# An encoder step on one core: the tiles whose v rows are gathered become 0 and 8, and the dense passes 1-3 and 4-7

## The chip, the cores and the metric

The kernel runs on one core of a Trainium2 chip. The metric is the device time of one execution in microseconds (us), the median of several runs. The profile is of one further execution of the same program.

## The reference, cut to what matters

One layer of a streaming encoder for 1024 prompt tokens and 64 sample tokens (the latter with 512 past ones), all in float32: a combined input projection, differential attention, multi-head latent attention (MLA), a gated merge, an output projection, and then a layer of single-neuron experts (PEER). The change concerns PEER. For each token it computes

```
s1, i1 = top_k(s[:, :, 0], 16); s2, i2 = top_k(s[:, :, 1], 16)
top, sel = top_k(s1[..., :, None] + s2[..., None, :], 16)
g = softmax(top)
act = gelu(einsum('td,thkd->thk', h, u[idx]))
out = einsum('thk,thkd->td', g * act, v[idx])
```

so that each token has 8 heads x 16 = 128 chosen experts out of 16384, a row of u (1024 numbers) for the dot product of each and a row of v for the weighted sum.

## The kernel before

Tokens are worked on in nine tiles: 0 to 7 are 128 prompt tokens each, tile 8 is the 64 sample tokens. Three groups (0 1 2, 3 4 5 and 6 7 8) run one after the other through projections, attention, MLA (48 units of a head and a tile in a group), the merge (w_b), w_out and PEER's scores (w_pq). Group 0 splits its matmul operands in two rounded halves; groups 1 and 2 run them in float32.

PEER's remaining work is cut into jobs, Python generators that give up control behind each step:

- route (28 steps): the top 16 of a tile's scores, on VectorE; writes the expert numbers and the gates to HBM.
- dots (128 steps, 64 for tile 8): per step one gather of 128 rows of u (`gather`, an indirect DMA that GpSimd issues, line 312) and one multiply-and-sum on VectorE (line 335). Ends with gelu and the weights (wgtd).
- build (33 steps): for a tile whose v is multiplied densely, one-hot products per eight tokens: two one-hot comparisons (375, 376) and two products on VectorE (384), eight scaled copies on ScalarE (381), 24 matmuls (391), two copies out of PSUM (395, 397). They make the tile's 128 x 16384 matrix of weights, in HBM (Ad), and for one tile (TR) 9 of 16 parts in SBUF (Ares). Each of its buffers has one copy.
- vg (128 or 64 steps): for a tile in VGATHER, per step one gather of 128 rows of v and one multiply-add on VectorE (line 426).

Jobs stand in two queues, r and d. `pump(us)` is called beside the matmuls (2.6 or 3.9 per projection piece; 1.1 to 1.16 times 1 + half the key blocks per attention or MLA unit; X) and gives each queue us x rate credits; a whole credit takes one step. So the rates set where in the program a step stands. Group 1 holds 577 us of pump (MLA 296 to 483, w_b to 515, w_out to 546, w_pq to 577), and group 2 holds 658 (q projection 140 to 172, attention to 292, MLA 323 to 564, then the same three); pass 0 holds 499. These positions are called credits below. The d queue starts in group 1 when tile 0 is routed, at 41.6. A group's routes come into the r queue at its end. The order in which each engine then runs its instructions is settled when the program is built, by `TileContext(nc, schedule_with_timeline_sim=True)`, in which the place in the program serves as priority, and an instruction that is ready can stand ahead of earlier ones that aren't. Gathers draw on four buffers of the pool gp and, while cur["more"] is set (from the end of group 0 to the end of group 2 in program order), on three more.

Behind the groups come two dense passes, over tiles 0 1 2 and 3 4 5 6. A pass reads all of v in 16 parts, splits each into two rounded halves (lines 1151, 1153), splits each tile's weights likewise (1165, 1166), and sums three products per tile in PSUM (line 1172). Pass 1 has four tiles, which fill all eight PSUM banks, so no build runs in it. `need` (line 1130) takes every step out of the queues up to the builds of the next pass. In program order the d queue runs: dots and build of tiles 0 to 6, dots of 8 and 7, v gathers of 8 and 7. The d rate is 0.42 in the groups and 1.0 in the passes. Each finished tile is normalised and stored by `finish`; the last v-gathered tile's finish stands at the very end (cur["late"]).

Of the kernel before, what the change touches and what calls it, by code (L numbers as in the profile page):

```python
# [20 lines left out]
D = 1024  # L21
# [11 lines left out]
MAGIC = float(0x5F3759DF)  # L33
MSC = 96.0 ** -0.5
GROUPS = ((0, 1, 2), (3, 4, 5), (6, 7, 8))
PASSES = ((0, 1, 2), (3, 4, 5, 6))
VGATHER = (8, 7)
GN = 384
SLOT = 3072
NW = 3  # L40
# [1 line left out]
PB = 5  # L42
NB = 8
RC = 9
TR = 6
RATE_D2, RATE_R2 = 1.0, 0.41
PUMP_G = (1.1, 1.113, 1.158)
RATE_D_G = (0.42, 0.42, 0.415)
RATE_R_G = (0.7, 0.7, 0.623)
DEPTH_DIFF = (3, 2, 2)  # L50
DEPTH_MLA = (2, 2, 2)
# [7 lines left out]
def hybrid_tile(ctx: ExitStack, tc: tile.TileContext, A):  # L59
# [3 lines left out]
    def ld(out, in_):  # L63
        if out.dtype == F32R:
            out = out.bitcast(F32)
        if in_.dtype == F32R:
            in_ = in_.bitcast(F32)
        return SP.dma_start(out, in_)
# [68 lines left out]
    def tr(t):  # L137
        return 128 if t < 8 else 64
# [166 lines left out]

    def gather(src, idx):
        gturn[0] += 1
        if cur["more"] and gturn[0] % 7 % 2:
            gb = cur["more"].tile([128, D], F32, name="gm", tag="gm")
        else:  # L310
            gb = cur["gp"].tile([128, D], F32, name="gb", tag="gb")
        G.indirect_dma_start(out=gb, out_offset=None, in_=src, in_offset=bass.IndirectOffsetOnAxis(ap=idx, axis=0))  # L312
        return gb
# [4 lines left out]
    def dots_job(t):  # L318
        ns = 128 if t < 8 else 64
        eidx = bp.tile([128, 128], I32, name="beidx")  # L320
        gk = bp.tile([128, 128], F32, name="bgk", tag="bgk")
        h2 = bp.tile([128, D], F32, name="h2r")
        if t < 8:
            ld(eidx, eidxd[t])
            ld(gk, gkd[t])
            ld(h2, h2d[t * 128:t * 128 + 128])
        else:
            ld(eidx[:, :64], packed(eidxd[8]))
            ld(gk[:, :64], packed(gkd[8]))
            src = h2d[NP:]  # L330
            ld(h2, bass.AP(tensor=src.tensor, offset=src.offset, ap=[[0, 2], [D, 64], [1, D]]))
        act = bp.tile([128, 128], F32, name="act")
        for k in range(ns):
            gb = gather(A["peer_u"], eidx[:, k:k + 1])
            V.scalar_tensor_tensor(gb, gb, 1.0, h2, op0=ALU.mult, op1=ALU.mult, accum_out=act[:, k:k + 1])  # L335
            yield
        wgt = act
        S.activation(wgt[:, :ns], act[:, :ns], AF.Gelu)
        V.tensor_tensor(wgt[:, :ns], wgt[:, :ns], gk[:, :ns], op=ALU.mult)
        ld(wgtd[t, :, :ns], wgt[:, :ns])  # L340

    def build_job(t):
        src = bp.tile([128, 3, 128], F32, name="bsrc", tag="oh1")
        ld(src[:, 0, :], wgtd[t])
        ld(src[:, 1:3, :], efd[t])
        p = cur["ps"].tile([128, 512], F32, name="mm")
        pv = p.rearrange("p (a n) -> p a n", n=128)
        for i in range(3):
            PE.transpose(pv[:, i, :], src[:, i, :], ident)
        ixT = bp.tile([128, 2, 128], BF16, name="ixT")  # L350
        S.copy(ixT, pv[:, 1:3, :])
        aT = bp.tile([128, 128], F32, name="aT")
        S.copy(aT, pv[:, 0, :])
        a3 = bp.tile([128, 3, 128], BF16, name="a3")
        a3f = bp.tile([128, 128], F32, name="a3f")
        for i in range(3):
            V.tensor_copy(a3[:, i], aT)
            if i == 0:
                V.tensor_copy(a3f, a3[:, 0])
            if i < 2:  # L360
                V.tensor_tensor(aT, aT, a3[:, i], op=ALU.subtract)
        yield
        shp = [128, 4, 128, 2]
        iv = iota2[:, None, :, :].to_broadcast(shp)

        def over(row, tt):
            return row[:, tt:tt + 8].rearrange("p (g x) -> p g x", x=2)[:, :, None, :].to_broadcast(shp)

        n = RC if t == TR else 0
        for t0 in range(0, 128, 16):  # L370
            stage = bp.tile([128, 16, 4, 8, 4], F32, name="stage", tag="stage")
            for tt in range(t0, t0 + 16, 8):
                oh1 = bp.tile(shp, BF16, name="oh1", tag="oh1")
                oh2 = bp.tile(shp, BF16, name="oh2")
                V.tensor_tensor(oh1, iv, over(ixT[:, 1], tt), op=ALU.is_equal)  # L375
                V.tensor_tensor(oh2, iv, over(ixT[:, 0], tt), op=ALU.is_equal)  # L376
                w3 = bp.tile([128, 3] + shp[1:], BF16, name="w3")
                for i in range(3):
                    if i == 0:
                        for x in range(8):  # L380
                            S.activation(w3[:, 0, x // 2, :, x % 2], oh2[:, x // 2, :, x % 2], AF.Copy,  # L381
                                         scale=a3f[:, tt + x:tt + x + 1])
                    else:
                        V.tensor_tensor(w3[:, i], oh2, over(a3[:, i], tt), op=ALU.mult)  # L384
                for q in range(2):
                    p = cur["ps"].tile([128, 512], F32, name="mm")
                    pv = p.rearrange("p (a n) -> p a n", n=128)
                    for j in range(4):
                        x = 4 * q + j
                        for i in range(3):  # L390
                            PE.matmul(pv[:, j, :], lhsT=oh1[:, x // 2, :, x % 2], rhs=w3[:, i, x // 2, :, x % 2],  # L391
                                      start=i == 0, stop=i == 2)
                    pc = p.rearrange("p (t c i) -> p c i t", t=4, i=8)
                    if n:
                        S.copy(cur["Ares"][:, :, (tt + 4 * q) // 4], pc[:, :n])
                    if n < 16:
                        S.copy(stage[:, n:, (tt - t0) // 4 + q], pc[:, n:])
                    yield
            ld(Ad[t, :, n:, t0 // 4:t0 // 4 + 4], stage[:, n:])

    def finish(acc, nr, t):
        if t in VGATHER:
            y = gp.tile([128, D], F32, name="y", tag="gb")
        else:
            y = cur["p2"].tile([128, D], F32, name="y", bufs=1)
        row_norm(y[:nr], acc[:nr], cur["gfin"], D, y[:nr])
        ld(out_rows("y", t), y[:nr])

    def vgather_job(t):
        while "p2" not in cur:  # L410
            yield
        ns = 128 if t < 8 else 64
        eidx = bp.tile([128, 128], I32, name="beidx")
        wgt = bp.tile([128, 128], F32, name="vwgt", tag="bgk")
        acc = cur["p2"].tile([128, D], F32, name="gacc", bufs=1)
        if t < 8:
            ld(eidx, eidxd[t])
            ld(acc, x1d[t * 128:t * 128 + 128])
        else:
            ld(eidx[:, :64], packed(eidxd[8]))  # L420
            V.memset(acc[64:128], 0.0)
            ld(acc[0:64], x1d[NP:])
        ld(wgt[:, :ns], wgtd[t, :, :ns])
        for k in range(ns):
            gb = gather(A["peer_v"], eidx[:, k:k + 1])
            V.scalar_tensor_tensor(acc, gb, wgt[:, k:k + 1], acc, op0=ALU.mult, op1=ALU.add)  # L426
            yield
        if t == 8:
            oth = cur["gp"].tile([128, D], F32, name="gb", tag="gb")
            ld(oth[0:64], acc[64:128])  # L430
            V.tensor_tensor(acc[0:64], acc[0:64], oth[0:64], op=ALU.add)
        if t == VGATHER[-1]:
            cur["late"] = lambda: finish(acc, tr(t), t)
        else:
            finish(acc, tr(t), t)

    def route_job(t, s_of):
        nr = tr(t)
# [97 lines left out]
        V.reciprocal(gs[:nr], gs[:nr])  # L536
        V.tensor_tensor(gk[:nr], gk[:nr], gs[:nr, :, None].to_broadcast([nr, H, 16]), op=ALU.mult)
        ld(gkd[t, :nr], gk[:nr].rearrange("p h k -> p (h k)"))
        if t not in VGATHER:
            queues["d"] += [(("dots", t), dots_job(t)), (("build", t), build_job(t))]  # L540
        elif t not in GROUPS[-1]:
            queues["d"].append((("dots", t), dots_job(t)))
        if t == max(x for x in GROUPS[-1] if x < 8):
            for v in [x for x in VGATHER if x in GROUPS[-1]]:
                queues["d"].append((("dots", v), dots_job(v)))
            for v in VGATHER:
                queues["d"].append((("vg", v), vgather_job(v)))

    for g, tiles in enumerate(GROUPS):
        cur["g"] = g  # L550
# [550 lines left out]
        gctx.close()  # L1101
        if g == 0:
            wctx.close()
            cur["more"] = ph1.enter_context(tc.tile_pool(name="gm", bufs=3))
    cur["more"] = None
    ph1.close()
    p2 = ctx.enter_context(tc.tile_pool(name="p2", bufs=2, reuse_waits="tile"))
# [16 lines left out]
    gfin = p2.tile([128, D], F32, name="gfin", bufs=1)  # L1124
    ld(gfin, bcast_rows(A["norm_final"], D))
    cur["gfin"] = gfin

    def need(tiles):
        for t in tiles:
# [158 lines left out]
```

## Time and profile before

| | |
|---|---|
| median of 3 runs | 4605.68 us (4603.78 to 4608.89) |
| the profiled execution | 4599.36 us, of which the span is 4597.6 us |
| mean granted TensorE clock | 0.873 |
| busy: TensorE, VectorE, ScalarE, GpSimd | 3811.5, 3301.5, 1680.1, 1993.2 us |
| gathers | 1280, of which 192 of v |

PE is TensorE (PEld its weight loads), DVE VectorE, ACT ScalarE, POOL GpSimd. A busy time is that of at least one instruction running. PEclk is the granted TensorE clock as a share of 2.4 GHz. Lines are those of the kernel; times in a stretch count from the start of the span.

### The profile page before, as it was taken

The page shows a single profiled execution, that of the slowest core. Times are in us where ns is not written, and L with a number is a line of the kernel's source. Part 1 is how long each engine was busy: PE and PEld are TensorE (multiplying, and loading weights), DVE is VectorE, ACT ScalarE, POOL GpSimd, SP SyncE. Part 2 cuts the span into 40 slices and gives each one's busy share as a digit, 9 for nine tenths or more (in the row PEclk, how much of TensorE's full clock was granted, in tenths as well). Part 3 has the DMA queues.
Part 4 walks back from the last instruction along what each step waited for, and adds up shares of the span by engine and source line. Part 5 has one row for each costly group of instructions (what it writes and reads, how often), then busy time and mean ns, then how long its engine had stood idle before and what let it go on. Part 6 is the DMA issues. An engine that isn't in the chain of part 4 may idle for free. (4 is left out here: it accounts for less than half of the span.)

```text
span 4597.6 us, 56297 instructions
## 1 busy us (share of the span) xinstructions
PE 3811.5 (83%) x19017; PEld 2989.6 (65%) x19017; DVE 3301.5 (72%) x7224; ACT 1680.1 (37%) x3720; POOL 1993.2 (43%) x1353
## 2 busy tenths in 40 slices
PE   6998988986776798887759977799999546999996
PEld 6977886645555575655536755577777435888885
DVE  4043457977889624797867886399997887777886
ACT  3344631124244522125613442335545453223231
POOL 3412331555777200233455554014465446555553
PEclk9967999977787898988759988899999757999998
DMA  5421245997989533788888789669988988998996
GB/s 174 172 84 57 75 164 191 354 346 263 357 302 336 183 118 121 245 299 290 270 276 277 263 276 311 207 226 324 339 288 298 314 286 287 351 336 308 354 345 227
DMA packets 467592, 1183.16 MB, mean 257 GB/s; under 512 B 45352, under 2 KB 218888, under 8 KB 452584
## 3 DMA queue, kind: packets, MB, share of 16 engines
q0 software_dynamic: 184320, 671.17, 41.4%
q1 hardware_dynamic: 282984, 508.41, 32.0%
q8 instruction: 150, 2.46, 0.2%
q14 instruction: 138, 1.13, 0.1%
HBM read 1074.60 MB, written 104.56 MB: 256 GB/s over the span
## 5 line engine op out<-in xcount | busy, mean ns | idle before, releaser
L312 POOL DMA_INDIRECT gb<-in_peer_u,beidx x917 | 1267.9, 1383 | 1632.0 <-DVE gb L335 708.1
L335 DVE SCALAR_TENSOR_TENSOR gb<-gb,h2r 128x1024 f32<-128x1024 f32 x917 | 1109.2, 1219 | 251.6 <-DMA gb<-in_peer_u,beidx 231.3
L1172 PE MATMUL acc_ps<-vlo,ahi 128*128 128x512 f32 x1792 | 562.8, 397 | 17.2 <-DVE vlo L1153 17.1
L1172 PE MATMUL acc_ps<-vhi,alo 128*128 128x512 f32 x1792 | 563.3, 396 | 14.9 <-DVE alo L1166 14.8
L1172 PE MATMUL acc_ps<-vhi,ahi 128*128 128x512 f32 x1792 | 559.8, 396 | 5.3 <-ACT ahi L1165 4.2
L391 PE MATMUL mm<-w,oh 128*128 128x128 bf16 x2688 | 255.7, 252 | 231.7 <-DVE oh L375 107.2
L1172 PEld LDWEIGHTS acc_ps<-vlo,ahi 128*128 128x128 f32 x1792 | 338.7, 191 | 93.2 <-DVE vlo L1153 24.2
L1172 PEld LDWEIGHTS acc_ps<-vhi,alo 128*128 128x128 f32 x1792 | 339.1, 190 | 88.7 <-DVE alo L1166 18.7
L1172 PEld LDWEIGHTS acc_ps<-vhi,ahi 128*128 128x128 f32 x1792 | 340.5, 191 | 78.3 <-ACT ahi L1165 6.0
L312 POOL DMA_INDIRECT gb<-in_peer_v,beidx x192 | 287.8, 1499 | 228.5 <-DVE gacc L426 159.0
L391 PEld LDWEIGHTS <-oh 128*128 128x128 bf16 x2688 | 209.6, 114 | 263.3 <-DVE oh L375 159.9
L1151 ACT CAST vhi<-vraw 128x1024 fp32r<-128x1024 f32 x256 | 265.6, 1053 | 192.4 <-DMA vraw<-in_peer_v 120.3
L312 POOL DMA_INDIRECT gm<-in_peer_u,beidx x171 | 220.8, 1291 | 256.0 <-DMA beidx<-eidxd 104.1
L166 PE MATMUL mm<-h,wraw 128*128 128x384 f32 (+1 forms) x1024 | 320.5, 474 | 13.5 <-ACT gt L696 11.2
L381 ACT ACTIVATE w<-oh,a3f 128x128 bf16<-128x128 bf16 x896 | 279.3, 428 | 102.4 <-DVE oh L376 62.5
L1153 DVE TENSOR_TENSOR vlo<-vraw,vhi 128x1024 fp32r<-128x1024 f32 x256 | 304.6, 1213 | 5.6 <-ACT vhi L1151 5.6
L426 DVE SCALAR_TENSOR_TENSOR gacc<-gb,vwgt,gacc 128x1024 f32<-128x1024 f32 x192 | 246.2, 1282 | 82.4 <-DMA gb<-in_peer_v,beidx 71.5
L178 POOL TENSOR_TENSOR wlo<-wraw,whi 128x2048 fp32r<-128x2048 f32 (+1 forms) x42 | 186.7, 4447 | 263.4 <-ACT whi L177 257.8
L166 PEld LDWEIGHTS mm<-h,wraw 128*128 128x128 f32 x1024 | 199.1, 196 | 130.1 <-issue 13.3
L1165 ACT CAST ahi<-araw 128x1024 fp32r<-128x1024 f32 x103 | 107.6, 1048 | 468.0 <-PE acc_ps L1172 402.8
L166 PE MATMUL mm<-wraw,h 128*128 128x256 f32 (+1 forms) x960 | 229.8, 395 | 33.3 <-ACT vt L689 33.1
L166 PEld LDWEIGHTS mm<-wraw,h 128*128 128x128 f32 (+1 forms) x960 | 176.5, 189 | 73.7 <-ACT vt L689 35.7
(381 smaller groups left out, 7199.3 us busy)
## 6 DMA issues: line engine op xcount, KB each, us to landing
vraw<-in_peer_v SPq DMA_DIRECT2D x256, 512.0 KB
wraw<-in_w_in SPq DMA_DIRECT2D x66, 1024.0 KB
araw<-Ad SPq DMA_DIRECT2D x103, 512.0 KB
Ad<-stage SPq DMA_DIRECT2D x48, 1024.0 KB
gb<-in_peer_u,beidx POOLq DMA_INDIRECT x917
wraw<-in_w_a SPq DMA_DIRECT2D x12, 1024.0 KB
wraw<-in_w_b SPq DMA_DIRECT2D x12, 1024.0 KB
wraw<-in_w_out SPq DMA_DIRECT2D x12, 1024.0 KB
```

The source lines that it names most:

```text
L166: PE.matmul(out, lhsT=L[0], rhs=R[0], start=start, stop=stop)
L178: G.tensor_tensor(lo[:, :n], raw[:, :n], hi[:, :n].bitcast(F32), op=ALU.subtract)
L312: G.indirect_dma_start(out=gb, out_offset=None, in_=src, in_offset=bass.IndirectOffsetOnAxis(ap=idx, axis=0))
L335: V.scalar_tensor_tensor(gb, gb, 1.0, h2, op0=ALU.mult, op1=ALU.mult, accum_out=act[:, k:k + 1])
L381: S.activation(w3[:, 0, x // 2, :, x % 2], oh2[:, x // 2, :, x % 2], AF.Copy, scale=a3f[:, tt + x:tt + x + 1])
L391: PE.matmul(pv[:, j, :], lhsT=oh1[:, x // 2, :, x % 2], rhs=w3[:, i, x // 2, :, x % 2], start=i == 0, stop=i == 2)
L426: V.scalar_tensor_tensor(acc, gb, wgt[:, k:k + 1], acc, op0=ALU.mult, op1=ALU.add)
L1151: S.copy(hi, raw)
L1153: V.tensor_tensor(lo, raw, hi.bitcast(F32), op=ALU.subtract)
L1165: S.copy(av, rv)
L1172: PE.matmul(pst[t][:, ds], lhsT=L[:, i, :], rhs=R[:, ds], start=c == 0 and i == 0 and L is ahi and R is vb[i][0], stop=c == 15 and i == 7 ...
```

## The change

Tile 0 is no longer built and multiplied densely; its v rows are gathered instead, and tile 7 changes places with it. Passes are over 1 2 3 and 4 5 6 7. Tile 0's v job is queued behind tile 3's build, with index and weight tiles of its own, and draws its sum from cur["more"]; all of it is taken out of the queue before the pools of the groups close. Its sum goes to x1d, and is read and finished at the head of the passes. Tile 8's dots and v gathers follow behind tile 7's build. The extra gather buffers are two instead of three, used by every third gather; the d rate is 0.56 in the groups and 1.3 in the passes. Before the build of TR (now 7) the r queue is emptied.

```
--- before.py
+++ after.py
@@ -33,8 +33,8 @@
 MAGIC = float(0x5F3759DF)
 MSC = 96.0 ** -0.5
 GROUPS = ((0, 1, 2), (3, 4, 5), (6, 7, 8))
-PASSES = ((0, 1, 2), (3, 4, 5, 6))
-VGATHER = (8, 7)
+PASSES = ((1, 2, 3), (4, 5, 6, 7))
+VGATHER = (0, 8)
 GN = 384
 SLOT = 3072
 NW = 3
@@ -42,10 +42,10 @@
 PB = 5
 NB = 8
 RC = 9
-TR = 6
-RATE_D2, RATE_R2 = 1.0, 0.41
+TR = 7
+RATE_D2, RATE_R2 = 1.3, 0.41
 PUMP_G = (1.1, 1.113, 1.158)
-RATE_D_G = (0.42, 0.42, 0.415)
+RATE_D_G = (0.56, 0.56, 0.56)
 RATE_R_G = (0.7, 0.7, 0.623)
 DEPTH_DIFF = (3, 2, 2)
 DEPTH_MLA = (2, 2, 2)
@@ -305,7 +305,7 @@
 
     def gather(src, idx):
         gturn[0] += 1
-        if cur["more"] and gturn[0] % 7 % 2:
+        if cur["more"] and gturn[0] % 3 == 1:
             gb = cur["more"].tile([128, D], F32, name="gm", tag="gm")
         else:
             gb = cur["gp"].tile([128, D], F32, name="gb", tag="gb")
@@ -340,6 +340,8 @@
         ld(wgtd[t, :, :ns], wgt[:, :ns])
 
     def build_job(t):
+        if t == TR:
+            drain("r")
         src = bp.tile([128, 3, 128], F32, name="bsrc", tag="oh1")
         ld(src[:, 0, :], wgtd[t])
         ld(src[:, 1:3, :], efd[t])
@@ -407,12 +409,10 @@
         ld(out_rows("y", t), y[:nr])
 
     def vgather_job(t):
-        while "p2" not in cur:
-            yield
         ns = 128 if t < 8 else 64
-        eidx = bp.tile([128, 128], I32, name="beidx")
-        wgt = bp.tile([128, 128], F32, name="vwgt", tag="bgk")
-        acc = cur["p2"].tile([128, D], F32, name="gacc", bufs=1)
+        eidx = bp.tile([128, 128], I32, name="veidx")
+        wgt = bp.tile([128, 128], F32, name="vwgt")
+        acc = (cur["more"] or cur["p2"]).tile([128, D], F32, name="gacc", tag="gacc", bufs=1)
         if t < 8:
             ld(eidx, eidxd[t])
             ld(acc, x1d[t * 128:t * 128 + 128])
@@ -429,10 +429,10 @@
             oth = cur["gp"].tile([128, D], F32, name="gb", tag="gb")
             ld(oth[0:64], acc[64:128])
             V.tensor_tensor(acc[0:64], acc[0:64], oth[0:64], op=ALU.add)
-        if t == VGATHER[-1]:
+        if t == 8:
             cur["late"] = lambda: finish(acc, tr(t), t)
         else:
-            finish(acc, tr(t), t)
+            ld(x1d[t * 128:t * 128 + 128], acc)
 
     def route_job(t, s_of):
         nr = tr(t)
@@ -536,15 +536,13 @@
         V.reciprocal(gs[:nr], gs[:nr])
         V.tensor_tensor(gk[:nr], gk[:nr], gs[:nr, :, None].to_broadcast([nr, H, 16]), op=ALU.mult)
         ld(gkd[t, :nr], gk[:nr].rearrange("p h k -> p (h k)"))
+        queues["d"].append((("dots", t), dots_job(t)))
         if t not in VGATHER:
-            queues["d"] += [(("dots", t), dots_job(t)), (("build", t), build_job(t))]
-        elif t not in GROUPS[-1]:
-            queues["d"].append((("dots", t), dots_job(t)))
-        if t == max(x for x in GROUPS[-1] if x < 8):
-            for v in [x for x in VGATHER if x in GROUPS[-1]]:
-                queues["d"].append((("dots", v), dots_job(v)))
-            for v in VGATHER:
-                queues["d"].append((("vg", v), vgather_job(v)))
+            queues["d"].append((("build", t), build_job(t)))
+        if t == PASSES[0][-1]:
+            queues["d"].append((("vg", 0), vgather_job(0)))
+        if t == 8:
+            queues["d"].append((("vg", 8), vgather_job(8)))
 
     for g, tiles in enumerate(GROUPS):
         cur["g"] = g
@@ -1101,7 +1099,9 @@
         gctx.close()
         if g == 0:
             wctx.close()
-            cur["more"] = ph1.enter_context(tc.tile_pool(name="gm", bufs=3))
+            cur["more"] = ph1.enter_context(tc.tile_pool(name="gm", bufs=2))
+    drain("r", ("route", PASSES[0][-1]))
+    drain("d", ("vg", 0))
     cur["more"] = None
     ph1.close()
     p2 = ctx.enter_context(tc.tile_pool(name="p2", bufs=2, reuse_waits="tile"))
@@ -1124,6 +1124,10 @@
     gfin = p2.tile([128, D], F32, name="gfin", bufs=1)
     ld(gfin, bcast_rows(A["norm_final"], D))
     cur["gfin"] = gfin
+
+    xr = p2.tile([128, D], F32, name="araw")
+    ld(xr, x1d[0:128])
+    finish(xr, 128, 0)
 
     def need(tiles):
         for t in tiles:
```

## Rows read from the trace of the kernel before

**Rows 1.** Head of the page.

```profile
span 4597.6 us, 56297 instructions
```

**Rows 2.** Stretch; busy (count) of PE, PEld, DVE, ACT, POOL; clock, DMA share, GB/s.

```profile
2970.00:3621.00 651.00, 601.94 (x3127) 482.58 (x3127) 586.03 (x1392) 310.47 (x542) 276.28 (x149) 0.96 0.86 297
3621.00:3846.00 225.00, 88.19 (x726) 72.25 (x725) 191.44 (x347) 111.83 (x333) 111.62 (x87) 0.56 0.89 294
3846.00:4562.00 716.00, 704.72 (x3074) 580.31 (x3072) 558.75 (x576) 193.53 (x189) 408.05 (x277) 0.99 0.91 329
```

**Rows 3.** The gathers (line 312) by stretch: GpSimd busy and count.

```profile
740.00:1561.00 821.00, 492.94 (x384) 0.80 0.87 316
1561.00:1886.00 325.00, 0.00 (x0) 0.95 0.34 117
1886.00:2884.00 998.00, 487.65 (x384) 0.84 0.83 284
2884.00:3052.00 168.00, 0.00 (x0) 0.88 0.58 189
3052.00:3532.00 480.00, 246.44 (x128) 0.97 0.90 315
3400.00:3500.00 100.00, 72.25 (x26) 0.97 0.89 310
3621.00:3846.00 225.00, 111.62 (x87) 0.56 0.89 294
3846.00:4050.00 204.00, 120.25 (x85) 0.98 0.93 338
4050.00:4562.00 512.00, 287.79 (x192) 0.99 0.90 325
```

**Rows 4.** First one-hots of the builds (line 375), 16 a build, by stretch.

```profile
1360.00:1570.00 210.00, 10.22 (x15) 0.76 0.84 297
...
3588.00:3731.00 143.00, 11.01 (x16) 0.70 0.92 315
3731.00:3846.00 115.00, 10.97 (x16) 0.51 0.85 277
```

**Rows 5.** The dots (line 335) from pass 0 to pass 1.

```profile
2970.00:3846.00 876.00, 282.21 (x467) 0.86 0.87 296
```

**Rows 6.** Ends of MLA units (line 926) by stretch, groups 1 and 2.

```profile
1290.00:1341.00 51.00, 3.21 (x12) 1.00 0.80 280
1341.00:1577.00 236.00, 5.06 (x19) 0.76 0.83 294
1577.00:1646.00 69.00, 4.49 (x17) 1.00 0.15 45
2448.00:2695.00 247.00, 10.30 (x42) 0.96 0.80 266
2695.00:2748.00 53.00, 1.44 (x6) 0.76 0.84 290
```

**Rows 7.** Busy time of all engines: three stretches of the groups' tails.

```profile
1561.00:1886.00 325.00, 300.18 (x1435) 218.32 (x1436) 120.32 (x527) 87.15 (x221) 0.00 (x0) 0.95 0.34 117
1646.00:1797.00 151.00, 142.09 (x570) 98.09 (x568) 37.76 (x164) 18.64 (x36) 0.00 (x0) 0.97 0.43 158
2768.00:2954.00 186.00, 145.15 (x732) 103.99 (x731) 96.32 (x198) 48.35 (x125) 54.40 (x40) 0.89 0.72 246
```

**Rows 8.** The q projection's copies (line 708), groups 1 and 2.

```profile
946.00:986.00 40.00, 3.79 (x8) 0.99 1.03 412
2014.00:2105.00 91.00, 3.48 (x8) 0.76 0.78 270
```

**Rows 9.** Ends of attention units (line 798) in group 2.

```profile
2105.00:2250.00 145.00, 4.04 (x12) 0.79 0.85 280
2250.00:2305.00 55.00, 2.12 (x6) 0.76 0.80 265
```

**Rows 10.** Section 5 of the page: the v gathers' accumulation.

```profile
L426 DVE SCALAR_TENSOR_TENSOR gacc<-gb,vwgt,gacc 128x1024 f32<-128x1024 f32 x192 | 246.2, 1282 | 82.4 <-DMA gb<-in_peer_v,beidx 71.5
```

More of the change, by code (lines that the diff above doesn't have):

```diff
@@ L35 @@
 GROUPS = ((0, 1, 2), (3, 4, 5), (6, 7, 8))
-PASSES = ((0, 1, 2), (3, 4, 5, 6))
-VGATHER = (8, 7)
+PASSES = ((1, 2, 3), (4, 5, 6, 7))
+VGATHER = (0, 8)
 GN = 384
@@ L44 @@
 RC = 9
-TR = 6
-RATE_D2, RATE_R2 = 1.0, 0.41
+TR = 7
+RATE_D2, RATE_R2 = 1.3, 0.41
 PUMP_G = (1.1, 1.113, 1.158)
-RATE_D_G = (0.42, 0.42, 0.415)
+RATE_D_G = (0.56, 0.56, 0.56)
 RATE_R_G = (0.7, 0.7, 0.623)
@@ L307, in gather @@
         gturn[0] += 1
-        if cur["more"] and gturn[0] % 7 % 2:
+        if cur["more"] and gturn[0] % 3 == 1:
             gb = cur["more"].tile([128, D], F32, name="gm", tag="gm")
@@ L342, in build_job @@
     def build_job(t):
+        if t == TR:
+            drain("r")
         src = bp.tile([128, 3, 128], F32, name="bsrc", tag="oh1")
@@ L409, in vgather_job @@
     def vgather_job(t):
-        while "p2" not in cur:
-            yield
         ns = 128 if t < 8 else 64
-        eidx = bp.tile([128, 128], I32, name="beidx")
-        wgt = bp.tile([128, 128], F32, name="vwgt", tag="bgk")
-        acc = cur["p2"].tile([128, D], F32, name="gacc", bufs=1)
+        eidx = bp.tile([128, 128], I32, name="veidx")
+        wgt = bp.tile([128, 128], F32, name="vwgt")
+        acc = (cur["more"] or cur["p2"]).tile([128, D], F32, name="gacc", tag="gacc", bufs=1)
         if t < 8:
@@ L431, in vgather_job @@
             V.tensor_tensor(acc[0:64], acc[0:64], oth[0:64], op=ALU.add)
-        if t == VGATHER[-1]:
+        if t == 8:
             cur["late"] = lambda: finish(acc, tr(t), t)
         else:
-            finish(acc, tr(t), t)
+            ld(x1d[t * 128:t * 128 + 128], acc)
     def route_job(t, s_of):
@@ L538, in route_job @@
         ld(gkd[t, :nr], gk[:nr].rearrange("p h k -> p (h k)"))
+        queues["d"].append((("dots", t), dots_job(t)))
         if t not in VGATHER:
[L540 to L547, printed above, removed]
+            queues["d"].append((("build", t), build_job(t)))
+        if t == PASSES[0][-1]:
+            queues["d"].append((("vg", 0), vgather_job(0)))
+        if t == 8:
+            queues["d"].append((("vg", 8), vgather_job(8)))
     for g, tiles in enumerate(GROUPS):
@@ L1103, in hybrid_tile @@
             wctx.close()
-            cur["more"] = ph1.enter_context(tc.tile_pool(name="gm", bufs=3))
+            cur["more"] = ph1.enter_context(tc.tile_pool(name="gm", bufs=2))
+    drain("r", ("route", PASSES[0][-1]))
+    drain("d", ("vg", 0))
     cur["more"] = None
@@ L1126, in hybrid_tile @@
     cur["gfin"] = gfin
+    xr = p2.tile([128, D], F32, name="araw")
+    ld(xr, x1d[0:128])
+    finish(xr, 128, 0)
     def need(tiles):
```

## The prediction, made before the changed kernel was run

> **What bounds the kernel now.** I read the span first [rows 1], then the engines' busy time by stretch for the part behind the three groups [rows 2], then where each kind of tail work (gathers, dots, builds) runs [rows 3 to 5], and last what a build costs the stage that it falls into [rows 6 to 9]. In rows 2 the reader is to see three stretches: the first dense pass (2970 to 3621 us), 225 us in which TensorE is busy for 88 us and no dense matmul can start, and the second pass (3846 to 4562), in which TensorE is busy for 704.7 of 716 us. The gap is made by order: the second pass takes all eight PSUM banks, so every build must be over, and the last two builds run from 3588 to 3846, a lone one in 115 us [rows 4]. Ahead of it VectorE is the fullest engine: 586.0 of 651 us and 191.4 of 225 us [rows 2]. Rows 3 show two stretches with no gather at all, 1561 to 1886 and 2884 to 3052: the dots of three tiles are done there and the next routing isn't. The 192 v gathers all lie in the second pass, beside TensorE's own work.
>
> **What the planner's order means.** Gathers run far ahead of their due place: by the credits, tile 2's dots are due in group 2 (its steps 322 to 449 of the d queue), and rows 3 have all 384 gathers of tiles 0 to 2 over by 1561. Builds stay at their due place: tile 0's is due at credits 346 to 425 of group 1's 577, and MLA holds credits 296 to 483; its one-hots run from 1360 to 1570 [rows 4], inside MLA's 1290 to 1646 [rows 6]. So I place moved builds by credits and moved gathers by the first idle stretch.
>
> **The change part by part.** The number of gathers, dots, builds and dense matmuls stays; seven tiles are built and passed densely before and after. What moves:
>
> (a) Tile 0's build leaves group 1's MLA. Rows 6: 12 units take 51 us with gathers and no build, 17 units take 69 us with neither, so about 4.1 us each; the 19 under the build take 236 us. 236 - 19 x 4.1 = 158, so -158 us. The granted clock tells the same: 1.00 before and behind, 0.76 under the build, between the two levels of 1.2 and 2.4 GHz, with TensorE waiting. The other bound is half of it, -80, if the saved time only lets other waits through.
>
> (b) Tile 1's build is now due at credits 499 to 558 of group 1 (rate 0.56: 128 dots to 270, 128 to 499, then 33 steps), which is w_b's second half, w_out and w_pq. The nearest rows are tile 2's build in the same place of group 2: the stretch from w_b to w_pq takes 186 us there and 151 us in group 1 without a build [rows 7], and the last six MLA units take 53 us for 6 x 5.9 [rows 6], 35 + 18 = 53. I take +55; bounds 0 (VectorE is busy 37.8 of 151 us there) and +115, a lone build.
>
> (c) In group 2, tile 1's build leaves the q projection and the first attention units: 91 us against 40 [rows 8], and 12 units in 145 us against 6 in 55 [rows 9], 12 x (12.1 - 9.2) = 35; together -86. Tile 2's build takes credits 209 to 268 there, some 11 of the 24 units: 11 x 2.9 = +32. Net -54.
>
> (d) Tile 2's build leaves group 2's tail, -53 as in (b); tile 3's comes, at credits 497 to 556, inside MLA (323 to 564), over 59 / 15.05 = 3.9 heads (15.05 credits each, of three units), 11.7 units. Priced as in (a), 236 / 19 - 4.1 = 8.3 us a unit: +97. Bounds +53 (as the old one) and +158. Net +44.
>
> (e) The 128 v gathers of tile 0 and their 128 accumulations, 1.282 us each [rows 10], 164 us of VectorE, move into the groups. Cover: 1561 to 1886 has no gather, and VectorE is busy 120.3 of 325 us [rows 7]. Their index and weight tiles have names of their own, so they wait for tile 0's dots alone and for gather buffers. They don't slow MLA (4.2 us with gathers, 4.1 without), but tile 1's build now stands there too. Bounds 0 and +164; I take +40, nearer the rows that show cover. One buffer fewer (six for seven) stretches 384 gathers from 821 us [rows 3] to at most 821 x 7 / 6 = 958, which still ends before tile 3's routing at 1886: nothing waits.
>
> (f) Before pass 1 may start, the dots of tiles 6 and 7 (256) and the builds of tiles 4 to 7 must now be over; before, it was tile 6 alone and builds 3 to 6, but 233 dots ran there in fact (467 records, two to a dot), 105 of them of tiles 8 and 7 as filler [rows 5]. So VectorE has at least 23 x 1.3 = 30 us more in a stretch where it is the fullest engine: +30. Bounds: 777 + 30 us at full use would fit in 807 of 876 us, -69; the other end is rival B, +132. With the rate at 1.3 all four builds are due inside pass 0 (credits 98 to 495 of 499), so part of the gap goes into a longer pass 0; that moves time and saves none by itself.
>
> (g) In pass 1, 277 gathers [rows 3] become 128 (tile 8's dots and v rows). TensorE is at 704.7 of 716 us, so -10, bounds 0 and -11. The tail behind the last matmul keeps five finishes; tile 0's finish moves to the head of pass 0, a load, some ten small operations and a store beside dense work: nothing, and about 5 us if pass 0 waits for its buffer.
>
> Sum: -158 + 55 - 54 + 44 + 40 + 30 - 10 = -53 us, on a span of 4597.6, a profiled execution of 4599.4 us (6.3 below the median of the runs): 4552.7 us on the median.
>
> **A rule weighed at (f).** Rows 3: in pass 0 the 128 gathers of tile 6 keep GpSimd busy 1.93 us each, and 2.78 us in the worst 100 us, against 1.28 in the groups and 1.50 in pass 1. The Trainium skill (SBUF — State Buffer, "Who interferes with whom") says that a VectorE instruction with two SBUF inputs contends with a GpSimd instruction that reads SBUF, which speaks against moving tile 7's gathers in among the splits of pass 0. By that rule at its worst row, 256 x 2.78 = 712 us from 3052, then a build of 115, pass 1 would start at 3879, +33 for (f). The pass-1 row, with the same splits beside it, speaks against its being the whole cause.
>
> **Rivals.**
> A, the forecast: builds leave MLA in group 1, the stretch before pass 1 grows little. 4553, its own range 4468 to 4595.
> B, slower: tile 7's dots gate pass 1. If tile 6's dots keep their 480 us from 3052 [rows 3] and tile 7's run at the gap's pace (225 / 87 = 2.59 us, 331 us), they end at 3863, the last build at 3978: +132 in place of +30, so -53 + 102 = +49, 4655 us. It decides once pass 1 starts over 83 us later against pass 0's start than now. For it: routing still holds VectorE early in pass 0. Against it: 105 of the dots there were filler, and the rate of 1.3 puts these ahead of dense work.
> C: the v gathers aren't pulled ahead of tile 3's dots, as both draw on the same buffers. The part is then not done in idle time: 128 x 998 / 384 = 333 us later in group 2, of which 2884 to 3052 hides 168; the other 165 us hold 63 dots of tile 5, 82 us of VectorE in pass 0, and the accumulations cost group 2 half of 164 for my 40: -53 + 82 + 42 = +71, 4677 us.
> D, no change: tile 3's build costs group 2's MLA what tile 0's cost group 1's (+158 for +97): -53 + 61 = +8, 4614 us.
>
> **How the numbers follow.** A has 0.55, B 0.22, D 0.15, C 0.08. The predicted time is A's. The range leaves about one in ten at each end: down to (e) at nothing and (f) at -15, 4468; up to C, 4675. A measurement of this kernel tells about 0.2%, 9 us, from no change: faster 0.55 is A, same 0.15 is D, slower 0.30 is B and C.
>
> **What would show each step.** (a): 48 MLA units of group 1 in some 200 us, at a granted clock near 1.0. (b), (d): one-hots of three builds in w_out and w_pq of group 1, in the attention and in the late MLA of group 2. (e): v gathers between about 1500 and 1900; after 2300 is C. (f): the time from pass 0's first dense matmul to pass 1's, 876 now: 906 by A, over 960 is B. (g): pass 1 near 706. I am wrong if group 1's MLA still takes 340 us, if the v gathers lie in group 2, or if VectorE in pass 0 waits for tile 7's gathers.

## The result and the profile after

The changed kernel takes 5026.0 us (median of 4 runs, 5012.3 to 5034.5) against 4607.1 for the kernel before: a ratio of 1.0907 [1.0879, 1.0936]. It is slower by 419 us, and the time lies far above the range that the prediction gave (4468 to 4675). The profiled execution has a span of 5032.7 us.

The busy time by stretch, cut at the first dense matmul, the end of pass 0, the start of pass 1 and the last matmul. The columns are those of [rows 2], to which these lines answer.

```profile
span 5032.7 us, 56375 instructions
...
2839.00:3430.00 591.00, 556.23 (x2523) 447.28 (x2523) 553.83 (x1352) 220.57 (x284) 300.88 (x174) 0.98 0.91 328
3430.00:4313.00 883.00, 164.60 (x1328) 138.23 (x1327) 632.55 (x1078) 205.55 (x590) 492.70 (x400) 0.51 0.83 276
4313.00:5020.00 707.00, 701.67 (x3077) 578.24 (x3076) 314.58 (x297) 193.54 (x192) 94.15 (x63) 1.00 0.50 176
```

The first dense matmul is at 2839 us, 138 earlier than before. Pass 1 came out at 707, as forecast. The loss is in the middle line: 883 us pass between the passes in place of 225, TensorE is busy for 165 of them, and its granted clock is 0.51 (0.56 before), close to the lower of its two levels.

Group 1's MLA units (the ends of units, line 924 here), the same before (line 926), and the first one-hots of builds (line 377 here) in the same stretch:

```profile
1288.00:1540.00 252.00, 12.49 (x47) 0.92 0.88 313
...
1291.00:1645.00 354.00, 12.49 (x47) 0.84 0.69 244
...
1288.00:1540.00 252.00, 0.00 (x0) 0.92 0.88 313
```

No build stands there any more, and the units take 252 us for 354.

The gathers (line 312) by stretch, beside [rows 3]:

```profile
740.00:1557.00 817.00, 492.26 (x384) 0.84 0.86 311
1557.00:1828.00 271.00, 0.07 (x1) 0.97 0.47 156
...
2155.00:2490.00 335.00, 173.32 (x132) 0.82 0.84 282
2490.00:2849.00 359.00, 1.25 (x1) 0.93 0.34 113
2849.00:3600.00 751.00, 396.98 (x249) 0.88 0.89 318
3600.00:4313.00 713.00, 396.60 (x325) 0.50 0.83 273
```

Two things stand here that the forecast didn't have. The v rows of tile 0 (128 of the 132) come at 2155 us, behind tile 3's dots; 1557 to 1828 stays without gathers. And there is a second stretch with none, 2490 to 2849, although tiles 4 and 5 have been routed by 2001 us. So 573 dots run between the first dense matmul and pass 1 (249 + 325 gathers), where before 233 did [rows 5].

What released GpSimd at 2849 is seen in the order of time (start, duration, engine and line, tiles, and in brackets the idle time before):

```profile
2836.84 1.06 ACT L202 ACTIVATE y<-araw 128x1024 f32<-128x1024 f32 x1 [1.47 <-DMA araw<-x1d]
...
2848.25 1.21 DVE L335 SCALAR_TENSOR_TENSOR gb<-gb,h2r 128x1024 f32<-128x1024 f32 x1
...
2849.73 0.94 POOL L312 DMA_INDIRECT gb<-in_peer_u,beidx  x1 [358.49 <-DVE Ares L445]
...
2859.91 0.34 SPq L68 DMA_DIRECT2D out_y_p<-y  x1
```

Only four gathers of tile 4 had been issued by 2490, and one of their dot products run. The next gather follows the second dot product, and that product follows the first write of y in tile 0's finish, at the head of the passes. In between VectorE is busy for 123 of 356 us (2492 to 2848) and runs none of these dots, so their place in the order that was settled at the build is behind the head of the passes. The page names a routing instruction as releaser; it shares nothing with the gather. What does share something is y: for a gathered tile it is taken from the gather buffers (tag "gb").

Last, what the engines waited for in the gap, 3430 to 4313 (total, times, longest):

```profile
PE mm L351 <- DMA bsrc<-wgtd: 447.2, 3, 153.6
```

Three builds wait for their dots' weights, 447 us in all. Before, over 3622 to 3846:

```profile
PE mm L349 <- DMA bsrc<-wgtd: 5.5, 1, 5.5
```

### The profile page after: what moved, and what is told of

It reads as the page before. It is cut to its first block, busy times and chain, and to the rows that moved or that the text cites. A ratio compares the mean times of both kernels' runs of the same rounds, so it can differ in the third digit from the quotient of the medians.

```text
span 5032.7 us, 56375 instructions
## 1 busy us (share of the span) xinstructions
PE 3786.3 (75%) x19017; PEld 2983.1 (59%) x19017; DVE 3326.4 (66%) x7224; ACT 1678.0 (33%) x3718; POOL 1928.6 (38%) x1353
## 4 chain that ended last, share of the span: by engine, by line
PE 24%; issue 11%; DVE 9%; DMA 8%; POOL 6%; ACT 2%; POOLq 0%; SPq 0%; ACTq 0%; DVEq 0%
PE acc_ps L1176 13%; POOL gb L312 6%; PE mm L166 4%; DMA gb<-in_peer_u,beidx 3%; DVE gb L335 3%; DMA Ad<-stage 2%; PE mm L919 1%; DVE vlo L1157 1%; DMA gb<-in_peer_v,veidx 1%; PE mm L393 1%; ACT w L383 1%; PE tp L725 1%; PE mm L794 1%; DVE alo L1170 1%; ACT stage L399 1%
## 5 line engine op out<-in xcount | busy, mean ns | idle before, releaser
L312 POOL DMA_INDIRECT gb<-in_peer_u,beidx x917 | 1232.4, 1344 | 1323.0 <-DVE gb L335 600.8
L393 PE MATMUL mm<-w,oh 128*128 128x128 bf16 x2688 | 275.7, 267 | 317.8 <-DVE oh L377 104.1
L393 PEld LDWEIGHTS <-oh 128*128 128x128 bf16 x2688 | 230.9, 121 | 361.6 <-DVE oh L377 183.0
L1155 ACT CAST vhi<-vraw 128x1024 fp32r<-128x1024 f32 x256 | 268.4, 1054 | 157.2 <-DMA vraw<-in_peer_v 78.3
L1170 DVE TENSOR_TENSOR alo<-araw,ahi 128x1024 fp32r<-128x1024 f32 x103 | 125.3, 1217 | 280.3 <-ACT ahi L1169 278.3
L312 POOL DMA_INDIRECT gb<-in_peer_v,veidx x149 | 208.1, 1397 | 164.4 <-DVE gacc L426 123.4
```

What stands on the lines that cost most here:

```text
L1155: S.copy(hi, raw)
L1170: V.tensor_tensor(alo.rearrange("p i (q t) -> p i q t", t=4), rv, av.bitcast(F32), op=ALU.subtract)
```

## The experiments

A time is set against the kernel before as run on the same chip; 1% is 46 us. Where two experiments are compared, their ratios to it are.

### The gather buffers and y

**e1**: y of tile 0 from a tag of its own in p2.

```
 def finish(acc, nr, t):
-    if t in VGATHER:
+    if t in VGATHER and t != 0:
```

> The changed kernel, but tile 0's finish takes its output tile y from the pass pool p2 (tag y, as the dense tiles do) and not from the gather ring gb. Theory 1 (ring order): the buffers of one tag are handed out in program order, y of tile 0 stands in the ring ahead of tile 4's gathers and can't be written before the groups' pools close, so the dots of tiles 4 and 5 wait for the passes; with y elsewhere they run in group 2 again, the stretch from the first dense matmul of pass 0 to that of pass 1 falls from about 1460 us to 850 to 950, and the time to 4560 to 4660. Theory 2 (VectorE load: the dots of tiles 6 and 7, at the rate of 1.3, gate pass 1 whatever the ring does): no gather moves, 4950 to 5030.

4785.8 us, 1.0413 [1.0377, 1.0448]: 4.9%, 227 us, are gone. Tile 4's 128 gathers now run in group 2, where the changed kernel had four:

```profile
2473.00:2777.00 304.00, 170.45 (x128) 0.83 0.82 268
```

It missed the expected time all the same, and the stretch from pass 0's first dense matmul to pass 1's is 1124 us, not 850 to 950: 187 us of loss stay, so y is about half of the answer.

**e2, e3**: the kernel before, with an extra finish of tile 0 at the head of the passes (its output is written once more at the end), with y from the gather buffers (e2) and from p2 (e3).

```
+    xr = p2.tile([128, D], F32, name="araw")
+    ld(xr, x1d[0:128])
+    y0 = gp.tile([128, D], F32, name="y", tag="gb")      (e2)
+    y0 = p2.tile([128, D], F32, name="y", bufs=1)        (e3)
+    row_norm(y0, xr, gfin, D, y0)
+    ld(out_rows("y", 0), y0)
```

> The kernel before, with one finish of tile 0 added at the head of the passes (load, norm, store; the rows are overwritten later by the real ones), whose y is taken from the gather ring gb. Nothing else moves. Theory 1: the gathers of tiles 4 and 5 (those that stand behind y) fall out of group 2, no gather from about 2300 to 2900, and the time goes up by 300 to 500 us, 4900 to 5100. Theory 2: within 15 us of the kernel before, 4595 to 4625.

> The same added finish of tile 0 in the kernel before, its y from the pass pool p2. It prices the added work alone. Theory 1 and theory 2 both: within 15 us of the kernel before; over 100 us slower would mean that the added load and norm at the head of the passes cost, not the ring.

e2 takes 5046.5 us (one run), 448 more than before; e3 takes 4597.1, 0.999 [0.9971, 1.001]. One tag in one line decides it. In e2 the gathers stop for 843 us and start again behind y:

```profile
2786.48 0.94 POOL L312 DMA_INDIRECT gb<-in_peer_u,beidx  x1 [843.10 <-DVE Ares L445]
```

Shown is that the shared tag holds back the dots behind it in the program until the head of the passes. That it does so because y can't be written before p2 opens is argued: how the build's scheduler ties the two is not read from the trace.

### The queue place of the v rows

**e4**: e1, with tile 0's v gathers alone on the two "gm" buffers and all u gathers on "gb".

```
...
+        if own:
+            gb = own.tile([128, D], F32, name="gv", tag="gm")
-        if cur["more"] and gturn[0] % 3 == 1:
+        elif not own_more and cur["more"] and gturn[0] % 3 == 1:
...
-            gb = gather(A["peer_v"], eidx[:, k:k + 1])
+            gb = gather(A["peer_v"], eidx[:, k:k + 1], cur["more"])
```

> As the run with y in p2, and tile 0's v gathers take the two extra buffers for themselves (u gathers keep the four of gb), so that they don't stand behind tile 3's gathers in a shared ring. Theory 1: the v gathers now run from about 1350 in group 1, where GpSimd idled from 1561 to 1886, and the time is 20 to 80 us below the run with y in p2, 4500 to 4620. Theory 2: 4950 to 5030, as the dots of tiles 6 and 7 are where they were.

4793.7 us, 1.0437 [1.0405, 1.0469], no better than e1. The v gathers spread over 764 to 1877 and the last gather of tile 2's dots is issued 315 us later than in e1: buffers taken from one are missing to the other. It tells nothing of the queue place.

**e8**: e1, with v queued ahead of tile 3's dots.

```
-        if t == PASSES[0][-1]:
+        if t == 2:
             queues["d"].append((("vg", 0), vgather_job(0)))
```

> e1 with one place changed: tile 0's v rows are queued ahead of tile 3's dots (behind tile 2's build) and not behind them, so that in the ring of gather buffers they come before tile 3's gathers. Theory (buffers are given out in the order of the program, and v behind tile 3's dots leaves GpSimd's queue idle from 1557 to 1828 us): the v gathers run in that stretch, each later tile's dots end 200 to 300 us earlier, tile 5's dots return to group 2, and the kernel takes 4620 to 4720 us. Rival (the v products only take VectorE's time from group 1 where it is needed, and the dots of tiles 6 and 7 gate pass 1 in any case): 4770 to 4800 us.

4724.0 us, 1.0262 [1.0225, 1.0298]: 1.5%, 69 us, better than e1, 4 us above the theory's range and well below the rival's. All 128 v gathers lie in the stretch that was empty, and tile 5's dots are back in group 2 (2587 to 2866):

```profile
1552.00:1850.00 298.00, 156.82 (x128) 0.83 0.92 331
```

The gain is small because the v rows cost the group something where they now stand (e13 to e15). The edit also moves something else: what is taken out of the queue before the passes ends with tile 0's v job, so tile 3's build is no longer among it. Its one-hots run from 2939 us, at the head of pass 0, and no longer from 2587, in group 2's MLA (e13 looks at its price).

### Tile 7's dots before pass 1

**e6** (on e1) and **e10** (on e8): tile 7's build takes weights of zero and its dots run behind it, so tile 7's routed part is missing from the output.

```
+    def blank_job(t):
+        act = bp.tile([128, 128], F32, name="act")
+        V.memset(act, 0.0)
+        ld(wgtd[t], act)
+        yield
-        queues["d"].append((("dots", t), dots_job(t)))
+        queues["d"].append((("dots", t), blank_job(t) if t == 7 else dots_job(t)))
+        if t == 7:
+            queues["d"].append((("late dots", t), dots_job(t)))
```

> The kernel after with tile 0's y in a buffer of its own (as in e1, 4786 us), and tile 7's expert dots taken out from in front of its build: the build uses weights of zero, and the same dots are worked out behind it, so tile 7's routed part is left out of the output while the gathers and VectorE's work stay the same. Theory (tile 7's dots, gathers first, gate its build and so pass 1): pass 1 starts 150 to 260 us earlier than e1's 4064 us, and the kernel takes 4540 to 4640 us. Rival (what is late is the sum of VectorE's and GpSimd's work, which is moved and not removed): pass 1 starts earlier and the end moves by under 50 us, 4740 to 4790 us.

> The two edits of e8 and e6 together, on top of e1's: y of tile 0 in its own buffer, tile 0's v rows ahead of tile 3's dots, and tile 7's dots behind its build, which uses weights of zero (tile 7's routed part is left out of the output, the work is the same). Theory (three separate costs make up the loss: the ring through y, 240 us; v behind tile 3's dots, 62 us; tile 7's dots before pass 1, 166 us): 4724 - 166 = 4558 us, so 4520 to 4600 us, and pass 1 starts near 3750 to 3860 us. Rival (with v early the dots of tile 7 no longer cost much, or the dots put behind delay the v rows of tile 8 to the same end): 4640 to 4720 us.

e6 takes 4619.7 us (one run), 166 less than e1, and pass 1 starts at 3885 for 4064. e10 takes 4597.2, 0.9991 [0.9965, 1.0016], 2.7% or 125 us less than e8, and pass 1 starts at 3851 for 4004. The wait of a build for its dots in the gap before pass 1, in e1, e8 and e10, in this order:

```profile
PE mm L351 <- DMA bsrc<-wgtd: 224.7, 2, 159.9
```

```profile
PE mm L351 <- DMA bsrc<-wgtd: 134.1, 1, 134.1
```

```profile
PE mm L357 <- DMA bsrc<-wgtd: 4.5, 1, 4.5
```

That tile 7's dots gate pass 1 is shown: 134 us of waiting taken away give 125. The edit also takes tile 7's 128 dot products out from before pass 1; that VectorE's time alone was short there is unlikely, since in e8's gap it is busy for 235 of 317 us, but no run separates the two:

```profile
3687.00:4004.00 317.00, 67.48 (x549) 55.42 (x547) 234.65 (x410) 88.32 (x264) 171.14 (x137) 0.52 0.83 276
```

Time before the passes and time at the gate add up only in part, though: e10 was to come near 4558 and is 39 above.

**e13**: e10 with group 2's pacing at 0.66, since e10's pass 0 begins with tile 3's build still running. Dense matmuls (tile acc_ps) in e10 at the head of pass 0, and the same in the kernel before:

```profile
2946.00:3062.00 116.00, 25.93 (x96) 18.94 (x95) 0.00 (x0) 0.63 0.56 183
3062.00:3160.00 98.00, 70.39 (x289) 55.21 (x290) 0.00 (x0) 0.84 0.89 318
```

```profile
2977.00:3095.00 118.00, 112.01 (x459) 89.51 (x460) 0.00 (x0) 0.93 0.70 235
```

> e10 (4597 us; y of tile 0 in its own buffer, its v rows early, tile 7's dots behind its build with weights of zero, so tile 7's routed part is left out of the output) with group 2's pacing at 0.66 for 0.56: tile 3's build stands ahead of pass 0. In e10 pass 0 issued 96 dense matmuls in its first 116 us and took 738 us against 645 before. Theory (that build at the head of pass 0 is the last of the loss, 93 us, and costs about 55 us in the group in its place): 4540 to 4580 us, near the 4553 of the prediction. Rival (pass 1 waits for the builds of tiles 4 to 7 in any case, at 3851 us, so an earlier end of pass 0 only widens the gap): 4590 to 4610 us.

4588.7 us, 0.9974 [0.9956, 0.9993], 0.2% better than e10, with intervals that overlap. Pass 0 shrank from 738 to 649 us, as the theory had it, and pass 1 began at 3856, no earlier: the rival holds to 1 us, pass 1 waits for the builds.

### What the v rows cost in the group

**e14**, **e15**: e13 with tile 0's products 8 columns wide, and e13 without its v gathers and products.

```
+            w = 8 if t == 0 else D                                   (e14)
+            V.scalar_tensor_tensor(acc[:, :w], gb[:, :w], wgt[:, k:k + 1], acc[:, :w], ...)
-            queues["d"].append((("vg", 0), vgather_job(0)))          (e15)
+            queues["d"].append((("vg", 0), iter((None,) * 128)))
```

> e13 (4589 us) with tile 0's v products taken over 8 of the row's 1024 columns, so the other columns of tile 0's routed part are left out of the output (as is tile 7's whole routed part); the gathers of v, their order and the builds stay. Theory (the 133 us by which e13's stretch from group 1's last MLA unit to group 2's first is longer than in e5, 951 against 818, is VectorE's time for 128 wide products): that stretch falls to 800 to 850 us, the first dense matmul comes 100 to 150 us earlier than 2983, and the kernel takes 4440 to 4500 us. Rival (the gathers themselves cost it, by the DMA engines that the group's weights share): the stretch stays over 900 us and the kernel takes 4550 to 4600 us.

> e13 (4589 us) with no v gather and no product of tile 0 at all (128 empty steps keep the builds and dots where they stand), so the routed parts of tiles 0 and 7 are left out of the output. Theory after e14 (4549 us: 40 us for the products, and in 1560 to 1860 the gathers still fill 0.91 of the DMA engines beside w_b, w_out and tile 1's build, 0.53 in e5): the rest of the 133 us is the gathers' DMA time, so the stretch between the MLA units of groups 1 and 2 falls to 830 to 870 us and the kernel takes 4440 to 4490 us. Rival (the rest is where tile 2's build and tile 3's dots stand, not the gathers): the stretch stays over 910 us and the kernel takes 4520 to 4560 us.

e14 takes 4548.8 us, 0.9899 [0.9849, 0.9948]; e15 takes 4501.1, 0.9784 [0.9719, 0.9849]. So tile 0's v rows cost 1.9%, 87 us, of which the products are some 35 and the gathers some 53. By the intervals the sum is good to some 30 us either way, and the split is rough, with two runs each. Both forecasts of mine were off: e14 came out 1 us below its rival's range, with the stretch between the MLA units at 937 us as the rival had it, and e15 fell between its two ranges. The stretch from 1560 to 1860, behind group 1's MLA, in the columns of [rows 7], for e13, e14 and e15:

```profile
1560.00:1860.00 300.00, 203.90 (x1007) 145.77 (x1007) 251.12 (x486) 81.97 (x213) 152.55 (x126) 0.82 0.91 327
```

```profile
1560.00:1860.00 300.00, 221.44 (x1147) 161.17 (x1145) 134.97 (x606) 89.78 (x241) 118.25 (x124) 0.86 0.91 336
```

```profile
1560.00:1860.00 300.00, 261.71 (x1384) 191.47 (x1385) 167.09 (x715) 98.13 (x262) 17.04 (x14) 0.94 0.50 167
```

With the products narrow VectorE is at 135 of 300 us, less than in e15, and TensorE is still at 221 for 262. What stays high is the DMA share, 0.91 for 0.50. TensorE's longest waits in e14 are for the build's copies (line 405), which empty its PSUM tiles and are stored by DMA; in e15 they are short:

```profile
PE mm L399 <- ACT stage L405: 19.3, 2, 12.7
PE mm L166 <- ACT stage L405: 18.8, 4, 8.4
```

```profile
PE mm L166 <- ACT stage L405: 4.4, 2, 2.8
...
PE mm L399 <- ACT stage L405: 0.3, 1, 0.3
```

These copies wait in turn for their own stores (27.5 us in e14, 10.2 in e15). In e14's tail of group 1 (1540 to 1730) the gathers' queue alone takes more than half of the DMA engines, beside w_out's loads and tile 1's build's stores (packets, MB, share):

```profile
q0 software_dynamic: 12429, 45.27, 62.1%
q1 hardware_dynamic: 16710, 23.34, 34.1%
```

### Where a build stands, and the pacing

**e5**: the kernel before, with the pacing of groups 1 and 2 alone changed, so that tile 0's build falls due behind group 1's MLA.

```
-RATE_D_G = (0.42, 0.42, 0.415)
+RATE_D_G = (0.42, 0.29, 0.5)
```

> The kernel before, with VectorE's pacing in groups 1 and 2 alone changed (0.42 and 0.415 become 0.29 and 0.5): tile 0's build falls due in the tail of group 1 (its output projection and what follows) in place of its MLA, tile 1's build stays in group 2's MLA and tile 2's moves behind it. Tiles gathered and passes are those of before. My theory (a build costs most where it stands in the MLA units, 158 us by the terms of the prediction, and about 55 us in the tail): 4490 to 4560 us, and group 1's MLA units shorter by about 100 us than before's 354 us. Rival (a build of 200 us costs VectorE the same wherever it stands, and the groups end when VectorE's work ends): 4580 to 4620 us, with the MLA shorter and the tail longer by as much.

4485.6 us, 0.9731 [0.9691, 0.977]: 2.7% faster than the kernel before (110 us by the medians), 4 us below the theory's range. The trace is of its slowest run, 4511 us; the others took 4461 to 4491. Group 1's MLA units (line 926) and the one-hots of builds (line 375) in it and behind it:

```profile
1295.00:1556.00 261.00, 12.56 (x47) 0.90 0.85 300
...
1295.00:1556.00 261.00, 0.00 (x0) 0.90 0.85 300
1556.00:1753.00 197.00, 11.05 (x16) 0.94 0.47 155
```

The gain that the change has in group 1's MLA is that of moving a build out of it, not of removing one. The edit isn't confined to tile 0's build: tile 1's, in group 2, moves from the q projection and the first attention units (2041 to 2241) to the attention alone (2181 to 2383, not into the MLA as I had expected), and tile 2's stays in the tail.

**e11**: e8 with the pacing of the kernel before.

```
-RATE_D2, RATE_R2 = 1.3, 0.41
+RATE_D2, RATE_R2 = 1.0, 0.41
-RATE_D_G = (0.56, 0.56, 0.56)
+RATE_D_G = (0.42, 0.42, 0.415)
```

> e8 (4724 us) with VectorE's pacing of the kernel before: 0.42, 0.42, 0.415 in the groups and 1.0 in phase 2, in place of 0.56 and 1.3. Theory (the pacing decides where builds stand, and a build in MLA units is what costs): with the lower pacing VectorE's jobs come later, tile 2's build moves towards group 2's MLA units and more of the jobs are left to phase 2, so 4740 to 4830 us. Rival (the pacing hardly matters, since group 1's MLA units are free of builds at either one): 4700 to 4740 us.

4749.2 us, 1.0329 [1.0286, 1.0372]: 0.7% above e8, with intervals that overlap; it lies in the theory's range, and tile 2's build did move into group 2's MLA (2611 to 2795). The raised rates are worth little and don't cause the loss.

### Three gathered tiles

**e9**: e8 with tiles 0, 8 and 7 gathered and two passes of three tiles. **e12**: e9 with group 2's pacing at 0.66.

```
-PASSES = ((1, 2, 3), (4, 5, 6, 7))
+PASSES = ((1, 2, 3), (4, 5, 6))
-VGATHER = (0, 8)
+VGATHER = (0, 8, 7)
-TR = 7
-RATE_D2, RATE_R2 = 1.3, 0.41
+TR = 6
+RATE_D2, RATE_R2 = 1.0, 0.41
...
-        queues["d"].append((("dots", t), dots_job(t)))
+        if t < 7:
+            queues["d"].append((("dots", t), dots_job(t)))
...
-            queues["d"].append((("vg", 8), vgather_job(8)))
+            for v in (8, 7):
+                queues["d"].append((("dots", v), dots_job(v)))
+            for v in (8, 7):
+                queues["d"].append((("vg", v), vgather_job(v)))
```

> e8 with three gathered tiles in place of two: tiles 0, 7 and 8, dense passes 1 to 3 and 4 to 6, the dots and v gathers of tiles 8 and 7 at the end as in the kernel before, and VectorE's pacing before pass 1 as before. Tile 0's build and dense part are then saved and tile 7's dots no longer stand before pass 1. Theory (the change loses by what it puts before pass 1, while the group loses a build): 4450 to 4560 us, with the first dense matmul near 2840 to 2900 us and pass 1 of three tiles some 540 us. Rival (GpSimd's gathers become the bound: 128 more of some 1.5 to 2 us each somewhere): 4600 to 4750 us.

> e9 (gathered tiles 0, 7 and 8; 4544 us) with VectorE's pacing in group 2 at 0.66 for 0.56, so that tile 3's build stands ahead of pass 0 and not at its head, where e9's pass 0 took 746 us against 645 before. Theory (pass 0 waits for tile 3's build): pass 0 takes 640 to 680 us, the last dense matmul comes 30 to 60 us earlier, and the kernel takes 4480 to 4530 us. Rival (the end is set by VectorE's accumulation of the 256 v rows of tiles 8 and 7, which e9 finishes 248 us behind its last dense matmul, so time saved in pass 0 only lengthens that tail): 4535 to 4555 us.

e9 takes 4543.8 us, 0.9881 [0.9845, 0.9918]: 1.2% below the kernel before, in the theory's range, and slower than e5. e12 takes 4552.9, 0.989 [0.9865, 0.9915], where the rival put it. Pass 1 and what follows it in e12:

```profile
3734.00:4266.00 532.00, 529.35 (x2356) 436.60 (x2353) 418.43 (x512) 182.80 (x198) 269.41 (x181) 0.99 0.91 334
4266.00:4550.00 284.00, 0.00 (x0) 0.00 (x0) 193.32 (x200) 4.48 (x8) 173.10 (x143) 0.51 0.82 273
```

284 us of gathers and products stand alone behind the last matmul: here the v rows of tiles 8 and 7 set the end.

## Why the prediction was wrong

In steps of the ratio, from the kernel before to the changed one: the moved builds without any v rows -2.2% (-99 us, e15), tile 0's v gathers and products +1.9% (+87, e15 to e13), group 2's pacing, which puts tile 3's build at the head of pass 0, +0.2% (+8, e13 to e10, within their intervals), tile 7's dots before pass 1 +2.7% (+125, e10 to e8), v behind tile 3's dots, and tile 3's build back in group 2's MLA, +1.5% (+69, e8 to e1), y in the gather buffers +4.9% (+227, e1 to the changed kernel). Each was taken out with those ahead of it still there; in another order the shares would differ.

The terms that failed are (g)'s clause that tile 0's finish costs nothing (227 us), (f)'s price for tile 7's dots (125 us for 30), and (e)'s cover and place for the v rows (87 us for 40, and 69 for standing behind tile 3's dots). (a) and (c) were off too, and an effect of y hid it.

- **(a) to (d): near in sum by luck, wrong in parts.** The sum was -113, and the first dense matmul came 138 us earlier in the changed kernel. By stretches, in us against the kernel before (e15 has no v rows, and by its pacing tile 3's build stands in group 2's tail; in the other two the v rows of (e) stand for the most part in (c)'s stretch):

| stretch | forecast | changed kernel | e1 | e15 |
|---|---|---|---|---|
| up to group 1's MLA | 0 | -3 | -8 | -9 |
| group 1's MLA, (a) | -158 | -102 | -100 | -99 |
| from there to the end of w_pq, (b) | +55 | +48 | +50 | +50 |
| from there to group 2's MLA, (c) | -54 | +11 | +5 | +14 |
| from there to the first dense matmul, (d) | +44 | -92 | +16 | -47 |
| sum | -113 | -138 | -37 | -91 |

(a) was too large: I priced a unit without a build at 4.1 us, from 12 units beside gathers and 17 without, but 47 units take 252 us, 5.4 each, in a stretch that is full of gathers and in which VectorE is busy for 230 us. (b) was right for the build that it was made for; tile 0's, in e5, costs the same stretch 27. (c) did not come. What fits is that dots running ahead take the time that tile 1's build leaves, since 28 more gathers stand in this stretch, but no run tests it. Before and in e15:

```profile
1787.00:2449.00 662.00, 243.69 (x195) 0.81 0.77 264
```

```profile
1729.00:2405.00 676.00, 289.22 (x223) 0.79 0.81 280
```

(d) shows a gain in the changed kernel only because y holds its gathers back; in e1, where they run again, the stretch is 16 us longer, and group 2's MLA with tile 3's build in it is +72 (370 for 298), inside my bounds for that build. Gathers from the start of group 2's MLA, before, in the changed kernel and in e1:

```profile
2449.00:2977.00 528.00, 243.96 (x190) 0.89 0.78 262
```

```profile
2403.00:2839.00 436.00, 52.00 (x41) 0.95 0.41 136
```

```profile
2396.00:2940.00 544.00, 290.85 (x226) 0.86 0.85 288
```

- **(e): +40 forecast, 87 measured** at the best queue place. I took 1561 to 1886 as cover because GpSimd was idle there and VectorE busy for 120 of 325 us [rows 7]. The same row has a DMA share of 0.34, and I passed over it: the gathers raise it to 0.91 beside w_out, and TensorE falls from 262 to 204 us busy in 300. The term on buffers in (e) was right: with one fewer, the 384 gathers of tiles 0 to 2 take 817 us for 821. On top, the changed kernel issues v at 2155, behind tile 3's dots, in group 2, which the prediction named as a sign of being wrong; that is rival C's mechanism, which I gave 0.08 and priced at +124 over A, for 69 measured.
- **(f): +30 forecast, 125 measured.** Rival B, at +132, was right in mechanism and size: builds wait for tile 7's dots (forecast to end at 3863 and the last build at 3978, in e8 3844 for the last gather and 4000; pass 1 starts 1054 us behind pass 0 there, over the 960 that I gave as B's sign). My reason against it, that 105 of the dots there were filler, was false, since filler holds nothing up and tile 7's dots now hold up a build. With tile 7's dots out of the way pass 1 begins 873 us behind pass 0 (2983 to 3856, e13), as before. The rule of the Trainium skill that I weighed there (SBUF — State Buffer, "Who interferes with whom") does not explain it: the gathers keep GpSimd 396.6 / 325 = 1.22 us each in the changed kernel's gap, and tile 7's in e8 79.5 / 57 = 1.39 us beside pass 0's splits, less than pass 0's 1.93 before [rows 3]. The rule speaks of GpSimd instructions that read SBUF; whether issuing a gather is one, no run here tests. Nor does a run separate what paces tile 7's dots (358 us for 128 gathers in e8).
- **(g): pass 1 right, its last clause the costliest error.** Pass 1 takes 707 for a forecast of 706. But I gave "nothing, and about 5 us" to the finish of tile 0 at the head of pass 0, having asked who waits for its work and not who shares its buffers. It cost 227 us here and 448 in e2. No rival had it.

With (e) and (f) at their measured values and y at 227 us, the forecast's sum of -53 becomes -53 + 47 + 95 + 227 = +316; v's queue place adds 69, so +385 of the measured 419. Most of the rest is that the moved builds gave 99 us (e15) for the 123 of (a) to (d) and (g).

## What to carry over

When work is moved, list the tag of every buffer that it takes, and what later work takes the same tag: a buffer that can only be written in a later stage stops a run-ahead that no data ties to it. An idle stretch is cover only if the DMA engines are idle too for work that loads, and dots that were filler become a gate when a build reads them. Ask first whether the gain needs the change at all: here two pacing constants (e5) gave 2.7% without moving a tile.

## What was not expected

The price of a gather is paid beside the engine that issues it. With GpSimd busy for 118 and VectorE for 135 of 300 us (e14), neither of them full, 128 gathers and their narrow products still cost TensorE 40 us of work in that stretch (221 for 262), at a DMA share of 0.91, and most of it is waiting for copies of a build (38.1 us for 4.7) whose stores share the DMA engines. In group 1's MLA the gathers alone don't show this: 12 units take 51 us at a DMA share of 0.80 and 17 take 69 at 0.15 [rows 6]. Where units do slow beside gathers, 5.4 us each in the changed kernel, VectorE is nearly full as well, so the two aren't separated there.
